# A streaming trunk step: places of the attention stage on Trainium2 laid out anew, and the samples' merges due later

## The chip, the core and the metric

The kernel runs on one core of a Trainium2 chip. The metric is device time in microseconds of one execution. A core has five engines that each work through their own queue in order: TensorE (PE, with its weight loads listed apart as PEld), VectorE (DVE), ScalarE (ACT), GpSimd (POOL) and SyncE (SP), which here issues nearly all DMA transfers.

## What is computed

One layer of a hybrid trunk for two groups of requests with shared weights: a prompt of 1024 tokens and 8 samples of 16 tokens each, 1152 tokens in all, model width 1024. The reference, cut:

```python
h = rms_norm(x, norm_g) * (1 + scale) + shift
q, k, v, z_att, z_ssd, xbc, dt_raw, gates = split(h @ w_in)
q, k = rms_norm(q per head), rms_norm(k per head)
o_att = attend(q, k, v)          # prompt: own chunk of 64 and the 8 before; samples: cache of 512 and own 16
att_branch = (o_att * silu(z_att)) @ w_att_proj
xs, bm, cm = split(silu(causal_dwconv(xbc)))
y = ssd_scan(xs, softplus(dt_raw), a, bm, cm) + d_skip * xs
ssd_branch = rms_norm(y * silu(z_ssd)) @ w_ssd_proj
out = x + gate * ((sigmoid(g_att) * att_branch + sigmoid(g_ssd) * ssd_branch) @ w_out)
```

There are 16 attention heads of 64, with a bias by relative position, and 32 SSD heads of 64 in 4 groups, state 128. Outputs are y, the new keys and values, the last convolution inputs and the SSD states.

## The kernel before, in words

**Dense work.** Each dense product is done as three fp16 matmuls (high part by high part, high by low, low by high; L412, L413 and L415, or L465 to L467 for q, k and v) into fp32 accumulation. A *job* is one set of weight columns: 128 output channels by 1152 tokens take 72 matmuls of 384 columns. Job weights come from DRAM into a *raw* place (`w_ahead`, L308: up to four loads ahead), and are split into a high half (ScalarE, L330) and a low half (VectorE, L331) in weight places; `level` (L322) also sums their squares. Before, there are four raw places (`L_RAW`) and six weight places (`L_W`), so three jobs' halves can stand at once. `w_next` splits the next job inside the present one; `w_done` frees the places.

**Stages.** After the start, there are eight *attention units* (two heads each), then the SSD stage (4 groups, 16 head pairs), then the projections and the output. A unit's dense generator makes q, k and v for nine token tiles (`dense_tok`), then the gate z of the unit after it. Beside it run three more generators. `prelude` normalizes and transposes q and k (L962 for the prompt, L978 for the samples). `prompt` does the attention of the prompt in the six `ROUNDS` of L1082, each with products of earlier tiles first and then scores of new ones. `sample` (L1145) does the samples in two halves of four.

**One prompt tile.** Scores (L1115, TensorE) go to PSUM, to the one `s` tile or to two of three `g` banks. VectorE adds the bias and takes the minimum of the negated scores (L1013). ScalarE takes the exponentials (L1010). VectorE normalizes and splits into two fp16 halves (L1045, L1046). A DMA transposes them (L1052). TensorE multiplies with the values (L1070), and VectorE merges with the gate (L1121). A tile's scores lie in *score places* `S`, in pairs with a second pair for the transposed halves: ten in the attention layout and four more in the far region, 14 in all.

**One half of the samples.** Four key loads (L1158) into the four places `K`; scores (L1168, L1171); minimum, exponential, L1177; a copy that separates the 16-bit halves of the words (ScalarE, L1189); a DMA transpose (L1190); a merge of the halves on VectorE (L1192); products (L1201) with values loaded into the same places `K` (L1185); a copy, a transpose (L1213) and the merge with the gate (L1219).

**Places.** All tiles lie in one arena with hand-written layouts that overlap in time: `L_ATT` for attention, `L_SSD` and `L_HEAD` for the SSD stage and its head, `L_TAIL` for the end. Behind them, from `E0` on, lies a far region: in attention it holds the four halves of V (`L_V`) and four score places, and otherwise up to six places of 1184 columns (`L_MORE`) that SSD and tail tiles take first. `alloc` takes, of the places of a kind that no live tile overlaps, the one longest free; without one, the generator waits.

**What sets the order.** `run` (L796) interleaves the generators at build time. It keeps a planner's clock, which every `yield` of a cost moves on. `until` and `pause` are due times on that clock: the transposed weights of a prompt tile are due `TURN` = 9000 ns after their scores are ready, and the samples' merge L1192 `TURN` after its DMA. When a generator finds no place, the planner's clock moves without dense work. The build then orders each engine's instructions once more; those under `late` or `keep` stay in program order. Due times order the program; they are not waits on the chip.

```python
nc.scalar.activation(planes(pt, 0, 5), words(p, 0, 5), AF.Copy)                                            # L1189
dma(p.ap.bitcast(U16).rearrange("p (i k) -> p i k", k=P), pt.ap.bitcast(U16), transpose=True)              # L1190
yield from pause(TURN)
nc.vector.tensor_copy(words(pt, 0, 5), planes(p, 0, 5))                                                    # L1192
```

```python
if (lay is L_SSD or lay is L_HEAD or lay is L_TAIL) and tag == "T" or lay is L_HEAD and tag == "Y":         # L233
    try:
        return Buf(arena, arena.alloc(L_MORE, "T", cols), cols)
```

## Time and profile before

| | us |
|---|---|
| three runs | 1839.16, 1843.87, 1847.39 (median 1843.87) |
| the profiled execution, its own time | 1841.84 |
| its span, first to last instruction | 1839.7 |
| TensorE busy | 1770.4 |
| VectorE busy | 1229.7 |
| ScalarE busy | 958.6 |
| GpSimd busy | 330.0 |

The profile is of one execution. Its page gives, for each engine, the busy time and its share of the span, and then the span in 40 equal slices of 46 us: a digit is the busy share in tenths, and PEclk is the clock that was granted to TensorE, in tenths of full speed. A row of the waits names the engine and line that waited, what ended the wait, the sum, the number of times and the longest. A row of the timeline gives start, duration, engine, line, operation and count, and in brackets the idle time just before it with what ended it. A row of the windows gives the stretch, its length, the busy time of PE, PEld, DVE, ACT and POOL with instruction counts, then the granted clock, the DMA share and GB/s. L12 is line 12 of the kernel before. Matmuls overlap, so the distance from one start to the next, not the duration of a row, is what one costs.

### The profile page before, as it was taken

To read this page: it belongs to the slowest core of one execution; us is meant where nothing else is said; L and a number is where in the kernel's file an instruction comes from. 1 tells how busy PE (TensorE), PEld (TensorE's weight loads), DVE (VectorE), ACT (ScalarE), POOL (GpSimd) and SP (SyncE) were. 2 spreads that over 40 slices of the span, in tenths; PEclk is the share of its full clock that TensorE was granted. 3 is DMA by queue.
4 is the path that set the end of the run, shared out by engine and by line. 5 is a ranking of instruction groups with operands and counts; after the bars stand their busy time and mean duration, and the time that the engine had idled before them with its cause. 6 is when DMAs were issued, how large, how long until landed. Compare 5 with 4: busy or idle time off the path is not lost. (4 is left out here: it accounts for less than half of the span.)

```text
span 1839.7 us, 35020 instructions
## 1 busy us (share of the span) xinstructions
PE 1770.4 (96%) x13821; PEld 1105.9 (60%) x13821; DVE 1229.7 (67%) x2327; ACT 958.6 (52%) x1903; POOL 330.0 (18%) x624
## 2 busy tenths in 40 slices
PE   7999999999999969999999999999999999999998
PEld 3655555555555546666666667666666656666664
DVE  6466766767677766777676868677764635887732
ACT  8765645555465547644655566356554613334520
POOL 0232322213123101211312222222222110000000
PEclk9999999999999979999999999999999999999999
DMA  9258778678678665443444445334466952331331
GB/s 382 76 132 215 169 193 202 151 208 195 150 221 189 164 159 150 139 138 112 113 141 120 133 132 176 129 114 112 145 177 208 345 172 99 110 98 50 98 122 54
DMA packets 266566, 284.88 MB, mean 155 GB/s; under 512 B 199628, under 2 KB 200664, under 8 KB 266392
## 3 DMA queue, kind: packets, MB, share of 16 engines
q1 hardware_dynamic: 257432, 253.90, 49.6%
q0 software_dynamic: 8960, 28.65, 4.2%
q8 instruction: 110, 1.80, 0.4%
q14 instruction: 64, 0.52, 0.1%
HBM read 192.70 MB, written 43.66 MB: 128 GB/s over the span
## 5 line engine op out<-in xcount | busy, mean ns | idle before, releaser
L412 PE MATMUL d<-arena 128*128 128x384 f16 x2172 | 709.5, 327 | 3.7 <-DVE arena L1423 3.5
L415 PE MATMUL d<-arena 128*128 128x384 f16 x2172 | 709.2, 327 | 0.0
L413 PE MATMUL d<-arena 128*128 128x384 f16 x2172 | 709.2, 327 | 0.0
L415 PEld LDWEIGHTS <-arena 128*128 128x128 f16 x2280 | 223.1, 98 | 147.7 <-issue 1.8
L412 PEld LDWEIGHTS <-arena 128*128 128x128 f16 x2280 | 223.4, 98 | 144.7 <-issue 6.3
L413 PEld LDWEIGHTS <-arena 128*128 128x128 f16 x2280 | 223.2, 98 | 142.4 <-issue 5.1
L322 ACT ACTIVATE arena<-arena 128x1024 bf16<-128x1024 f32 (+3 forms) x169 | 181.8, 1076 | 144.3 <-DMA arena<-in_wall_dram 122.1
L330 ACT ACTIVATE arena<-arena 128x1024 f16<-128x1024 f32 (+1 forms) x117 | 122.1, 1044 | 175.5 <-PE d L413 149.3
L465 PE MATMUL d<-arena 128*128 128x384 f16 (+1 forms) x568 | 186.6, 329 | 1.9 <-ACT arena L668 1.6
L466 PE MATMUL d<-arena 128*128 128x384 f16 (+1 forms) x568 | 186.4, 329 | 0.0
L467 PE MATMUL d<-arena 128*128 128x384 f16 (+1 forms) x568 | 186.3, 328 | 0.0
L331 DVE SCALAR_TENSOR_TENSOR arena<-arena 128x1024 f16<-128x1024 f32 (+1 forms) x117 | 148.9, 1273 | 53.2 <-ACT arena L330 53.0
L1010 ACT ACTIVATE arena<-arena 128x640 f32<-128x640 f32 (+3 forms) x144 | 100.9, 703 | 122.4 <-DVE arena L1013 122.3
L1452 ACT ACTIVATE arena<-arena 128x128 f32<-128x128 f32 x288 | 88.6, 387 | 50.9 <-DMA arena<-acs_d 50.8
L1264 DVE SCALAR_TENSOR_TENSOR arena<-arena 128x1176 f32<-128x1176 f32 x72 | 104.6, 1453 | 12.2 <-ACT arena L1261 11.6
L1046 DVE SCALAR_TENSOR_TENSOR arena<-arena 128x640 f16<-128x640 f32 (+4 forms) x128 | 87.4, 713 | 0.0
L465 PEld LDWEIGHTS <-arena 128*128 128x128 f16 x576 | 56.3, 98 | 51.6 <-issue 17.5
L938 POOL TENSOR_SCALAR arena<-arena 128x16 f32<-128x16 f32 (+1 forms) x24 | 7.5, 312 | 423.0 <-DVE arena L911 422.1
L467 PEld LDWEIGHTS <-arena 128*128 128x128 f16 x576 | 56.4, 98 | 37.4 <-issue 0.3
L466 PEld LDWEIGHTS <-arena 128*128 128x128 f16 x576 | 56.5, 98 | 35.6 <-issue 2.3
L1514 POOL TENSOR_TENSOR rarena<-rarena,arena 128x256 fp32r<-128x256 f32 x64 | 55.3, 878 | 73.8 <-PE g L1598 50.2
L1534 DVE SCALAR_TENSOR_TENSOR arena<-arena,g 128x64 f32<-128x64 f32 x224 | 46.4, 275 | 32.6 <-ACT arena L1530 30.6
(242 smaller groups left out, 2621.0 us busy)
## 6 DMA issues: line engine op xcount, KB each, us to landing
arena<-in_wall_dram SPq DMA_DIRECT2D x85, 512.0 KB
arena<-acs_d SPq DMA_DIRECT2D x32, 576.0 KB
arena<-in_kc_dram SPq DMA_DIRECT2D x64, 256.0 KB
arena<-in_vc_dram SPq DMA_DIRECT2D x64, 256.0 KB
arena<-in_wada_dram SPq DMA_DIRECT2D x24, 512.0 KB
arena<-in_xT_dram SPq DMA_DIRECT2D x16, 576.0 KB
arena<-eacs_d SPq DMA_DIRECT2D x32, 288.0 KB
gate_d<-arena POOLq DMA_DIRECT2D x48, 192.0 KB, 3.1
```

The costliest lines, as they stand in the source:

```text
L322: keep(nc.scalar.activation(junk[:, :n], x, AF.Square, scale=scale * n ** -0.5, accum_out=sums[:, c:c + 1]))
L330: keep(nc.scalar.activation(hi, x, AF.Copy, scale=scale))
L331: keep(nc.vector.scalar_tensor_tensor(lo, x, scale, hi, ALU.mult, ALU.subtract))
L412: nc.tensor.matmul(ps, hi.r[:, wc], kh.r[:, tok], start=k == 0, stop=False)
L413: nc.tensor.matmul(ps, hi.r[:, wc], kl.r[:, tok], start=False, stop=False)
L415: nc.tensor.matmul(ps, lo.r[:, wc], kh.r[:, tok], start=False, stop=k == nk - 1)
L465: nc.tensor.matmul(ps, kh.r[:, tok], wh, start=k == 0, stop=False)
L466: nc.tensor.matmul(ps, kh.r[:, tok], wl, start=False, stop=False)
L467: nc.tensor.matmul(ps, kl.r[:, tok], wh, start=False, stop=k == KT - 1)
L1010: nc.scalar.activation(p, p, AF.Exp, bias=sm_[:, 4 + e:5 + e], scale=-1.0, accum_out=sm_[:, 6 + e:7 + e])
L1264: nc.vector.scalar_tensor_tensor(yc, r.ap[:, j:j + n], w4[:, i, j:j + 1], yc, ALU.mult, ALU.add)
L1452: nc.scalar.activation(me[e].ap[:, cs], me[e].ap[:, cs], AF.Relu, scale=-1.0, bias=a4[:, c, hds[e]:hds[e] + 1])
```

## The change

From L226 on, line numbers are four higher in the changed kernel. The diff, with what only renumbers the layout left in:

```diff
@@ layouts (L199 to L225) @@
-    H0 = fixed[0] + 4 * 1024
+    NSLOT = 12
+    H0 = fixed[0] + 3 * 1024
-    V0 = W0 + 6 * 512
+    V0 = W0 + 4 * 512
-    E0 = Z0 + 2 * 1024 + 5 * NT + 12 * 640 + 4 * 512 + 2 * 256 + 2 * 128 + 3 * 84
+    E0 = Z0 + 2 * 1024 + 5 * NT + (NSLOT + 2) * 640 + 4 * 512 + 4 * 256 + 3 * 128 + 3 * 84
-    L_RAW = arena.set_layout(fixed[0], [("raw", 4, 1024)])
+    L_RAW = arena.set_layout(fixed[0], [("raw", 3, 1024)])
-    L_W = arena.set_layout(W0, [("w", 6, 512)])
+    L_W = arena.set_layout(W0, [("w", 4, 512)])
-    L_ATT = arena.set_layout(Z0, [("Q", 1, 16 * P), ("T", 5, NT), ("S", 10, 640), ("U", 2, 640), ("K", 4, 512), ("q", 1, 256), ("d", 1, 256),
-                                  ("k", 1, 128), ("p", 1, 128), ("n", 2, 36 + 3 * 16), ("t", 6, 14)])
+    L_ATT = arena.set_layout(Z0, [("Q", 1, 16 * P), ("T", 5, NT), ("S", NSLOT, 640), ("U", 2, 640), ("K", 4, 512), ("q", 2, 256), ("d", 2, 256),
+                                  ("k", 2, 128), ("p", 1, 128), ("n", 2, 36 + 3 * 16), ("t", 6, 14)])
-    L_MORE = arena.set_layout(E0, [("T", 6, 1184), ("H", 1, 1024)])
+    L_MORE = arena.set_layout(E0, [("T", 3, 1184), ("H", 1, 1024)])
+    n = (HCOLS - E0 - 3 * 1184 - 1024) // 1184
+    L_MORE["T"] = L_MORE["T"] + arena.set_layout(E0 + 3 * 1184 + 1024, [("T", n, 1184)])["T"]
     L_SSD["H"] = L_SSD["H"] + L_MORE["H"]
-    L_V = arena.set_layout(E0, [("v", 4, NP // 2)])
-    L_ATT["S"] = L_ATT["S"] + arena.set_layout(E0 + 4 * NP // 2, [("S", 4, 640)])["S"]
+    L_V = arena.set_layout(E0, [("v", 2, NP // 2), ("pad", 1, 160)])
+    L_V["v"] = L_V["v"] + arena.set_layout(E0 + 1184, [("v", 2, NP // 2)])["v"]
+    L_ATT["Q"] = L_ATT["Q"] + arena.set_layout(E0 + 1184 + NP, [("Q", 1, 2048)])["Q"]
@@ w_ahead (L308) @@
-        while not hold[0] and loaded[0] < len(parts) and len(wraw) < 4:
+        while not hold[0] and loaded[0] < len(parts) and len(wraw) < 3:
@@ sample (L1191) @@
-                yield from pause(TURN)
+                yield from pause(TURN + 4000)
```

In numbers, n comes out as 4. `Q`, where a unit's q and k of eight token tiles stand until they are transposed, gets a second place, in the far region behind V. Score places go from 14 (ten and four far ones) to twelve. The places `q`, `d` and `k` of `L_ATT` go from one to two. Raw places go from four to three, and loads ahead with them; weight places go from six to four, two jobs' halves. The far region's dense places go from six to seven; beside attention, those that neither V nor the score places nor the second Q overlap go from two to four. The planner's due time of the merge L1192 goes from 9000 to 13000 ns after its DMA. No instruction is added or removed on any engine; the planner and the ordering at build time place them anew.

## The prediction

> **What bounds the kernel now.** I read the page first: which engine fills the span, and in which slices it does not.

> ```profile
> PE 1770.4 (96%) x13821; PEld 1105.9 (60%) x13821; DVE 1229.7 (67%) x2327; ACT 958.6 (52%) x1903; POOL 330.0 (18%) x624
> PE   7999999999999969999999999999999999999998
> PEclk9999999999999979999999999999999999999999
> ```

> TensorE is busy for 96% of the span. Its work is the same after the change (the same matmuls stand in both programs as built, in another order), so the change can move only the idle 4% and the time at a lower clock. Both digits dip in one slice, the fifteenth. So next I read busy time by stretch: attention units 0 to 6, the end of the last unit, the SSD stage, the end.

> ```profile
> 60.00:620.00 560.00, 542.37 (x5046) 319.62 (x5043) 386.36 (x1023) 317.29 (x770) 147.70 (x298) 1.00 0.71 174
> 620.00:680.00 60.00, 41.95 (x416) 26.21 (x416) 43.60 (x100) 31.62 (x64) 5.09 (x12) 0.80 0.72 171
> 700.00:1450.00 750.00, 738.93 (x5521) 494.95 (x5520) 527.79 (x794) 416.95 (x788) 166.26 (x291) 1.00 0.48 146
> 1490.00:1830.00 340.00, 340.00 (x2102) 204.16 (x2099) 202.29 (x316) 109.63 (x145) 0.00 (x0) 1.00 0.29 95
> ```

> The first number after the length is TensorE's busy time. Idle: 17.6 us in units 0 to 6, 18.0 us in the 60 us at the end of attention, 11.1 us in the whole SSD stage, none after. Third, who ended these waits (TensorE's waits, for 100 to 620 and then for 620 to 680):

> ```profile
> PE s L1115 <- DVE arena L1013: 6.3, 6, 1.3
> PE g L1201 <- DVE arena L1192: 6.1, 6, 1.7
> PE s L1168 <- DMA arena<-in_kc_dram: 2.6, 4, 0.9
> ...
> PE g L1070 <- DMA arena<-arena: 0.8, 2, 0.5
> ```

> ```profile
> PE g L1070 <- DMA arena<-arena: 9.9, 4, 5.6
> PE g L1070 <- DVE arena L1013: 3.7, 1, 3.7
> PE s L1168 <- issue: 2.2, 1, 2.2
> PE g L1213 <- DVE arena L1121: 1.3, 1, 1.3
> ```

> In the units, scores (L1115) wait for VectorE to read the bank before, and the samples' products (L1201) for the merge L1192. At the end, the products L1070 wait for transposed weights. Fourth, the timeline: TensorE at that end, then VectorE in unit 1.

> ```profile
> 655.44 3.41 PE L1070 MATMUL g<-arena 128*64 128x128 f16 x60 [3.67 <-DVE arena L1013]
> 658.78 0.98 PE L1115 MATMUL s<-arena 64*128 64x320 f16 x6
> 659.56 1.01 PE L1115 MATMUL g<-arena 64*128 64x320 f16 x6
> 660.77 1.25 PE L1168 MATMUL s<-arena 128*32 128x512 f32 x4 [0.21 <-DVE arena L1013]
> 667.65 0.28 PE L1070 MATMUL g<-arena 128*64 128x128 f16 x1 [5.63 <-DMA arena<-arena]
> 673.24 0.31 PE L1070 MATMUL g<-arena 128*64 128x128 f16 x1 [2.44 <-DMA arena<-arena]
> 674.33 1.81 PE L1070 MATMUL g<-arena 128*64 128x128 f16 x29 [0.78 <-DMA arena<-arena]
> ```

> ```profile
> 202.50 0.89 DVE L1192 COPY arena<-arena 128x1280 uint16<-128x1280 uint16 x1 [4.75 <-DMA arena<-arena]
> 203.28 0.33 DVE L1013 CUSTOM_DVE_ANT_0 arena<-s,arena 128x128 f32<-128x128 f32 x1
> ```

> The last unit has run out of dense matmuls to put between scores and products: from the last scores (660.57) to the last weights (674.33) is 13.8 us of latency with nothing to cover it. In the units, L1192 stands at the head of VectorE's queue until its transpose lands; the L1013 that TensorE needs stands behind it.

> **The change, part by part.** For dense work I use 0.163 us a matmul:

> ```profile
> 647.68 0.33 PE L413 MATMUL d<-arena 128*128 128x384 f16 x1
> 649.30 0.33 PE L415 MATMUL d<-arena 128*128 128x384 f16 x1
> ```

> There are ten starts between them, 1.62 us. Distances come from TensorE's order as built, durations from this trace.

> *Places (L_MORE, L_V, second Q).* Beside attention, the head of the SSD stage could take only the two dense places of the far region that V and the four extra score places leave free; now it is four. In the order as built this shows in unit 7. Before, round 3's scores are followed by round 4's products without a dense matmul, and round 4's scores by round 5's products likewise. After, 52 dense matmuls stand ahead of the first half of round 4's products, 22 more ahead of the rest, and 83 (20 and 63) between round 4's scores and round 5's products: 83 x 0.163 = 13.5 us, with the samples' scores 15.9, against the 13.8 needed. In full units the same place has 84. So I take 15 of the 18.0 idle us as gone, 3 as left. Bounds: all gone; or half, if what is late next (the transposes, behind loads in SP's queue) grows by what the cover gains.

> With the idle time goes the lower clock:

> ```profile
> 620.00:630.00 10.00, 7.78 (x47) 4.02 (x47) 6.56 (x17) 7.29 (x16) 2.10 (x7) 0.85 0.50 132
> 650.00:660.00 10.00, 5.03 (x74) 4.16 (x73) 9.56 (x21) 4.51 (x7) 0.00 (x0) 0.72 0.98 234
> 660.00:670.00 10.00, 3.11 (x31) 1.33 (x27) 7.03 (x18) 2.90 (x7) 0.00 (x0) 0.67 0.78 185
> 670.00:680.00 10.00, 6.78 (x63) 4.36 (x60) 4.67 (x8) 4.91 (x13) 1.48 (x4) 0.59 0.82 189
> ```

> ```profile
> 676.36 0.53 PE L413 MATMUL d<-arena 128*128 128x384 f16 x1
> 676.68 0.53 PE L415 MATMUL d<-arena 128*128 128x384 f16 x1
> ```

> At 676 dense matmuls start 0.32 us apart, twice the 0.163. If clock is full or half, 0.85, 0.72, 0.67 and 0.59 are 3.0, 5.6, 6.6 and 8.2 us at half. TensorE worked through the first (3.0) and about two thirds (20.4 of 30) of its 14.9 us in the others: 13 us of work at half, so 6.5 us lost. I take 5 as regained, 1.5 as lost again in a gap that stays.

> [...]

> *Merges later (TURN + 4000).* The planner's due time of L1192 moves 4 us back, and with it all behind it in the samples' chain: 20 product steps (L1201), their copy and transpose, the release of four K places and of a U place, and so the four key loads of the next half on SP.

> ```profile
> DVE arena L1192 <- DMA arena<-arena: 54.3, 16, 5.0
> ```

> VectorE stood 54.3 us at 16 merges. As built, the first half's merge now stands behind at least the four L1013 that free the score bank in units 1 to 6 (before: ahead of all six), so the 6.3 us of L1115 waits should go. The second half's merge has moved past little more than one instruction and still stands ahead of L1121 and the next unit's L1013; its products have 15.3 to 21.2 us behind their scores, against 14.3 in units 0 to 5. Of those 6.1 us I take half, since the next scores now stand where these products stood. Cost of the moved key loads:

> ```profile
> 222.53 1.30 SPq L1158 DMA_DIRECT2D arena<-in_kc_dram  x3
> 228.25 0.62 PE L1168 MATMUL s<-arena 128*32 128x512 f32 x1 [0.59 <-DMA arena<-in_kc_dram]
> ```

> Last load to arrival is 4 to 5 us, and units 1 and 4 now leave about 6 us between the second half's products and the next samples' scores, where 15 stood. Bounds 0 and 4 us a unit; I take 1.

> *Twelve score places, pairs of q, d, k.* They let units run in another rhythm: dense work is spread unevenly. Scores of round 0 to products of round 2 have 8.3 and 9.5 us of TensorE work in units 1 and 4 (before 17.0), and round 1 to round 3 9.8 and 8.8 in units 3 and 6 (before 19.9). The trace shows no such short distance in a full unit. Bounds: nothing, as the products are spread over the arrivals (in unit 1 the 36 stand in four pieces between samples' scores); or the 13.8 us above less the distance: 5.5, 4.3, 4.0 and 5.0 in the four units, 19. I take 5, nearer to nothing, as query tiles 0 to 3 have one to four key blocks where tile 7, of the 13.8, has five.

> *Fewer weight and raw places.* A split then starts when the job before ends, one job later. Cover:

> ```profile
> 1148.63 1.06 ACT L330 ACTIVATE arena<-arena 128x1024 f16<-128x1024 f32 x1 [1.11 <-PE d L413]
> 1156.15 1.22 DVE L331 SCALAR_TENSOR_TENSOR arena<-arena 128x1024 f16<-128x1024 f32 x1
> ```

> Of the stage's 54 splits, paired row by row, this is the slowest from start to end, 8.7 us; a job lasts 72 x 0.163 = 11.7. Cost nothing. If the cover went, each late split would cost its lateness. Three raw places still load two jobs or more ahead.

> *SSD stage.* One place more, and as built the pairs stand evenly inside a group, most with 78 to 81 dense matmuls between them where 114 to 138 stood, and about 200 at group ends. VectorE has 527.8 us of work there in 750. I take 0; bounds -8 (most of the 11.1 us idle) and +10.

> Sum, against the profiled execution (1841.84, the span of 1839.7 and 2.1 around it; the runs' median is 1843.87): end of attention -15 - 5, waits at the merges -6.3 - 3, key loads +2, uneven units +5, SSD 0: -22. **1820 us.**

> **The rivals.**

> 1. *Uneven units wait.* The new short distances cost their upper bound, 19 instead of 5, and the key loads theirs, 8 instead of 2. For it: VectorE and SP work in order, and the DMA share is 0.71 there. Against: L1070 waited 0.8 us for transposes in all units 0 to 6, so 17.0 us of cover was ample. 1820 + 20 = 1840; at half the price, 1830.

> 2. *The end only moves.* Transposes queue behind loads (DMA share 0.98 at 650 to 660) and half the tail stays: 1820 + 10 = 1830. The change would then not do at the end what its places allow.

> 3. *Slower: weights late.* With two jobs' places, a split cannot hide behind two jobs. It decides when a split takes more than 11.7 us after the previous job. If VectorE's queue, fuller inside the closer pairs, adds 5 us to the 8.7 (four of its 1.3 us rows), a split is 2.0 us late; 20 of the 54 in the stage so, 40 us: 1860.

> ```profile
> L331 DVE SCALAR_TENSOR_TENSOR arena<-arena 128x1024 f16<-128x1024 f32 (+1 forms) x117 | 148.9, 1273 | 53.2 <-ACT arena L330 53.0
> L330 ACT ACTIVATE arena<-arena 128x1024 f16<-128x1024 f32 (+1 forms) x117 | 122.1, 1044 | 175.5 <-PE d L413 149.3 <-PE g L413 24.1 <-DMA arena<-in_wall_dram 1.5
> ```

> Against it: the two operations alone take 1.04 + 1.27 = 2.3 us, and ScalarE already waits 149.3 us for TensorE with the split, so it comes as soon as it may.

> **How the numbers follow.** Forecast 0.55; uneven units 0.20; the end only moves 0.12; weights late 0.13. Low end: both bounds at the good side, all of the tail (-24), all waits at merges (-12.4), nothing added: 1805, with a little of the SSD idle 1803. High end: rival 1 at its price and the SSD stage 2 us worse, 1842. That leaves out rival 3 and little else. A measurement of this kernel can tell about 0.5%, 9 us, from no change. Faster by more (below 1834.7): the forecast, half of rival 1, most of rival 2, 0.73. Within: 0.14. Slower: 0.13.

> **What would show it.** In the profile after, the fifteenth slice should be 9 for TensorE and clock, and 13 us between the last L1115 and the last L1070 of unit 7 should be full of d matmuls. L1115 should no longer wait for L1013 by 6 us; VectorE's 54.3 us at L1192 should be halved. Wrong if L1070 waits for the transposes by over 10 us in units 1, 3, 4, 6, or if d matmuls wait for L331 in the SSD stage.

## The result, and the profile after

The changed kernel takes **1855.69 us** (median of 20 runs, 1844.99 to 1864.97), the kernel before 1845.67 beside it (20 runs, 1839.16 to 1851.43): a ratio of 1.0053, 95% interval 1.0039 to 1.0067. It is 10 us slower; the forecast was 1820, and the range ended at 1842. The profiled execution of after took 1858.02 us with a span of 1856.2, against 1841.84 and 1839.7: these two differ by 16.5 us of span, since before's lies 4 us under its median and after's 2 us above.

TensorE's row and the two rows of slices of after:

```profile
PE 1774.5 (96%) x13821; PEld 1105.0 (60%) x13821; DVE 1225.4 (66%) x2327; ACT 957.6 (52%) x1903; POOL 362.6 (20%) x624
PE   7999998999989989999999999999999999999998
PEclk9999999999999999999999999999999999999999
```

TensorE is busy for 4.1 us more than before with the same matmuls, and idle for 12.4 us more. The dip of the fifteenth slice is shallower, 8 for 6, and the clock's digit there is 9 for 7; but the seventh and the twelfth slice have gone from 9 to 8. By stretch (units 0 to 6; the next 60 us; the SSD stage; the end):

```profile
60.00:620.00 560.00, 527.80 (x4880) 310.47 (x4879) 365.58 (x973) 304.19 (x742) 163.94 (x287) 0.98 0.71 170
620.00:680.00 60.00, 53.30 (x506) 31.37 (x505) 54.24 (x137) 33.03 (x72) 9.13 (x24) 0.97 0.66 159
700.00:1450.00 750.00, 729.27 (x5440) 487.08 (x5438) 520.50 (x788) 413.90 (x793) 174.14 (x290) 0.99 0.48 146
1500.00:1840.00 340.00, 340.00 (x2101) 204.25 (x2100) 206.06 (x320) 115.59 (x153) 0.00 (x0) 1.00 0.30 100
```

Idle in units 0 to 6: 32.2 us where 17.6 stood. At the end of attention 6.7 where 18.0 stood, at a clock of 0.97 where 0.80 stood. In the SSD stage 20.7 where 11.1 stood. So the end did get better, and more was lost on both sides of it. TensorE's waits in 100 to 620:

```profile
PE g L1074 <- DMA arena<-arena: 14.6, 11, 2.7
PE g L1205 <- DVE arena L1196: 5.9, 2, 3.8
PE g L1119 <- DVE arena L1223: 2.4, 2, 1.6
PE g L1074 <- DVE arena L1125: 2.2, 1, 2.2
```

Line numbers are four higher: L1074 is L1070, the products that wait for transposed weights: 0.8 us before, 14.6 now. The waits of L1119 (L1115 before) for L1017 (L1013), 6.3 us, are gone from the list. One such wait, in unit 2 (units are counted from 0, each from its first scores), on SP, then VectorE, then TensorE (`...` where rows are left out):

```profile
266.98 2.88 SPq L1194 DMA_TRANSPOSE arena<-arena  x1
272.92 0.33 SPq L1158 DMA_DIRECT2D arena<-in_bias_s_dram  x1
274.77 1.24 SPq L1056 DMA_TRANSPOSE arena<-arena  x1
276.12 0.52 SPq L316 DMA_DIRECT2D arena<-in_wall_dram  x1
276.73 1.24 SPq L1056 DMA_TRANSPOSE arena<-arena  x1
```

```profile
267.65 0.16 DVE L1042 RECIPROCAL arena<-arena 128x2 f32<-128x2 f32 x1
272.00 0.90 DVE L1196 COPY arena<-arena 128x1280 uint16<-128x1280 uint16 x1 [4.19 <-DMA arena<-arena]
272.79 0.15 DVE L1043 TENSOR_SCALAR arena<-arena 128x2 f32<-128x2 f32 x1
...
273.18 0.87 DVE L1049 TENSOR_SCALAR arena<-arena 128x512 f16<-128x512 f32 x2
273.97 0.74 DVE L1050 SCALAR_TENSOR_TENSOR arena<-arena 128x512 f16<-128x512 f32 x1
```

```profile
281.62 1.21 PE L1074 MATMUL g<-arena 128*64 128x128 f16 x23 [2.66 <-DMA arena<-arena]
...
284.77 0.53 PE L470 MATMUL d<-arena 128*128 128x384 f16 x1
285.09 0.44 PE L471 MATMUL d<-arena 128*128 128x384 f16 x1
```

The later merge (L1196, L1192 before) still stands on VectorE until its transpose lands, 4.19 us. Only what is behind it is another thing now: the normalization (L1042, L1043, L1049, L1050) of the tile whose weights TensorE needs next; its first instruction had run at 267.65, the next one runs at 272.79. The transposes leave at 274.77 and 276.73, and TensorE stands for 2.66 us. Behind the gap dense matmuls start 0.32 us apart, at half clock.

This wait and one of 2.33 us in unit 5 are the only two of the eleven with a merge that held VectorE for over 4 us in the 9 us before their transpose left. Both are at round 3's products, with 13.3 us of TensorE work behind round 1's scores where 18.0 stood before (worked out from the order, by the usual times of the next section). Of the 14.6 us, round 3 has 5.0, all in units 2 and 5, and round 4 has 8.2, in units 1, 3 and 4.

### The profile page after: what moved, and what is told of

It is laid out like the page before. It is cut to its first block, busy times and chain, and to the rows that moved or that the text cites. A ratio compares the mean times of both kernels' runs of the same rounds, so it can differ in the third digit from the quotient of the medians.

```text
span 1856.2 us, 35017 instructions
## 1 busy us (share of the span) xinstructions
PE 1774.5 (96%) x13821; PEld 1105.0 (60%) x13821; DVE 1225.4 (66%) x2327; ACT 957.6 (52%) x1903; POOL 362.6 (20%) x624
## 4 chain that ended last, share of the span: by engine, by line
PE 44%; DMA 7%; DVE 6%; ACT 5%; issue 2%; SPq 0%; POOL 0%; DVEq 0%; ACTq 0%; POOLq 0%
PE d L416 12%; PE d L417 12%; PE d L419 12%; DMA arena<-arena 3%; DMA arena<-acs_d 3%; ACT arena L1456 2%; DVE arena L1488 1%; DVE arena L1268 1%; PE g L416 1%; PE g L419 1%; PE g L417 1%; PE s L1557 1%; PE g L1529 1%; PE g L1577 1%; DVE arena L335 1%
## 5 line engine op out<-in xcount | busy, mean ns | idle before, releaser
L416 PEld LDWEIGHTS <-arena 128*128 128x128 f16 x2280 | 223.9, 98 | 152.5 <-issue 14.3
L417 PEld LDWEIGHTS <-arena 128*128 128x128 f16 x2280 | 223.7, 98 | 148.4 <-issue 11.6
L326 ACT ACTIVATE arena<-arena 128x1024 bf16<-128x1024 f32 (+3 forms) x169 | 181.8, 1076 | 195.2 <-DMA arena<-in_wall_dram 155.6
L334 ACT ACTIVATE arena<-arena 128x1024 f16<-128x1024 f32 (+1 forms) x117 | 121.9, 1044 | 153.2 <-PE d L417 124.6
L335 DVE SCALAR_TENSOR_TENSOR arena<-arena 128x1024 f16<-128x1024 f32 (+1 forms) x117 | 143.5, 1229 | 79.7 <-ACT arena L334 79.4
L1050 DVE SCALAR_TENSOR_TENSOR arena<-arena 128x640 f16<-128x640 f32 (+4 forms) x128 | 90.5, 735 | 0.0
L1017 DVE CUSTOM_DVE_ANT_0 arena<-s,arena 128x320 f32<-128x320 f32 (+4 forms) x128 | 58.8, 501 | 26.3 <-PE s L1175 15.5
L1074 PE MATMUL g<-arena 128*64 128x128 f16 x1440 | 52.2, 223 | 23.4 <-DMA arena<-arena 19.5
```

The lines of the kernel that those rows point to most:

```text
L326: keep(nc.scalar.activation(junk[:, :n], x, AF.Square, scale=scale * n ** -0.5, accum_out=sums[:, c:c + 1]))
L334: keep(nc.scalar.activation(hi, x, AF.Copy, scale=scale))
L335: keep(nc.vector.scalar_tensor_tensor(lo, x, scale, hi, ALU.mult, ALU.subtract))
L416: nc.tensor.matmul(ps, hi.r[:, wc], kh.r[:, tok], start=k == 0, stop=False)
L417: nc.tensor.matmul(ps, hi.r[:, wc], kl.r[:, tok], start=False, stop=False)
```

## The experiments

A measure for all of them. In each kernel I take the time at which TensorE reaches a landmark (the first scores of unit 0 and of unit 7, the first L1525 of the first and of the last SSD pair), less the usual start-to-start times of all matmuls ahead of it in the order as built (0.163 us for a dense one, and so on from the trace of before). What a stage adds to this difference is its *loss*: idle time, half clock, matmuls that don't overlap. It is worked out from one execution: a_n3 has TensorE's order of after up to 704 us, and the two differ by 8 us in the units. So the medians carry the verdicts. Kernels are named by their labels; "ratio" is to the kernel before, in the same set of runs; in these sets the median of the kernel before went from 1843.68 to 1846.55. The last three columns are losses in us.

| kernel | edit | median us | ratio (95%) | loss, units 0-6 | loss, end | loss, SSD |
|---|---|---|---|---|---|---|
| before | | 1845.67 | | 25.3 | 25.5 | 8.7 |
| after | the change | 1855.69 | 1.0053 (1.0039-1.0067) | 47.0 | 12.9 | 16.8 |
| b_far | before + far region | 1835.56 | 0.9949 (0.9930-0.9967) | 31.8 | 11.6 | 10.0 |
| b_turn | before + later merges | 1853.60 | 1.0044 (1.0027-1.0061) | 31.9 | 28.4 | 10.4 |
| b_w4 | before + fewer weight places | 1848.96 | 1.0020 (1.0009-1.0030) | 33.9 | 23.4 | 9.6 |
| a_qdk1 | after, single q, d, k | 1846.53 | 0.9998 (0.9983-1.0013) | 29.5 | 17.3 | 12.1 |
| a_n3 | after, six far places | 1848.70 | 1.0016 (1.0004-1.0027) | 38.8 | 12.0 | 9.1 |
| a_noturn | after, early merges | 1832.66 | 0.9935 (0.9923-0.9946) | 27.4 | 4.8 | 17.4 |
| a_qdk1_n3 | a_qdk1 and a_n3 together | 1841.22 | 0.9985 (0.9973-0.9997) | 31.6 | 17.5 | 9.4 |
| a_qdk1_noturn_n3 | the same, early merges | 1830.86 | 0.9927 (0.9914-0.9940) | 30.2 | 15.3 | 4.4 |
| a_noturn_n3 | early merges, six far places | 1841.64 | 0.9979 (0.9964-0.9995) | 27.2 | 16.1 | 11.5 |
| a_qdk1_noturn | single q, d, k, early merges | 1857.31 | 1.0067 (1.0051-1.0084) | 29.9 | 14.8 | 31.1 |
| a_noQ_noturn_n3 | a_noturn_n3, one Q | 1836.79 | 0.9947 (0.9931-0.9963) | 23.7 | 14.8 | 16.3 |
| a_noQ_qdk1_noturn_n3 | and single q, d, k | 1830.16 | 0.9910 (0.9893-0.9927) | 32.1 | 16.0 | 4.9 |
| a_turn06 | after, early merge in unit 7 | 1868.51 | 1.0107 (1.0092-1.0122) | 48.3 | 12.1 | 32.5 |
| a_turn7 | after, early merges in 0 to 6 | 1831.44 | 0.9917 (0.9898-0.9935) | 32.8 | 7.4 | 11.4 |
| a_qdk1_noturn_lev | a_qdk1_noturn, squares from the split half | 1839.20 | 0.9955 (0.9941-0.9969) | 32.3 | 9.8 | 16.3 |
| a_lev | after, the same | 1852.60 | 1.0039 (1.0026-1.0053) | 42.1 | 10.7 | 20.2 |
| a_noturn_lev | a_noturn, the same | 1834.23 | 0.9945 (0.9929-0.9961) | 23.2 | 15.0 | 17.0 |
| a_best_lev | a_noQ_qdk1_noturn_n3, the same | 1817.51 | 0.9866 (0.9842-0.9890) | 23.5 | 13.2 | 1.1 |

The row "before" is of one execution. b_far and b_turn have its order of TensorE in units 0 to 6 and lost 31.8 and 31.9 there: so before's 25.3 is a good execution of its kind, and about 32 is the fairer number to compare with.

**The parts alone.** b_far, the far region in another order:

```diff
-    L_MORE = arena.set_layout(E0, [("T", 6, 1184), ("H", 1, 1024)])
+    L_MORE = arena.set_layout(E0, [("T", 3, 1184), ("H", 1, 1024)])
+    L_MORE["T"] = L_MORE["T"] + arena.set_layout(E0 + 4 * NP // 2 + 4 * 640, [("T", 3, 1184)])["T"]
```

> The kernel before with the far region alone laid out in another order (three T places, H, three more T places behind V and the four score places), so that three instead of two dense places stay free beside attention; everything else as before. As built, units 0 to 6 keep TensorE's order of before and unit 7 gets dense matmuls ahead of rounds 4 and 5 (16.4 and 4.5 us of TensorE work between scores and products where 9.8 and 0.9 stood). Theory F (the free far places alone repair the end of attention, as step 1 of the prediction had it): idle at the end of attention falls from 18.0 to about 8 us, the clock there rises, SSD stage nearly unchanged (pairs 38 to 50 us apart as before): 12 us faster than before (6 to 18), about 1833. Rival E (the end only moves: a later start of the first SSD pairs gives back what attention gains): within 4 us of before.

Theory F holds: 1835.56, half a per cent faster than before. The stretch 620 to 700 in before and in b_far:

```profile
620.00:700.00 80.00, 61.95 (x575) 37.90 (x575) 50.76 (x109) 39.73 (x78) 7.39 (x16) 0.85 0.65 159
```

```profile
620.00:700.00 80.00, 69.59 (x668) 42.21 (x666) 56.16 (x122) 46.76 (x94) 8.76 (x19) 1.00 0.82 200
```

Idle 18.05 to 10.4 us, clock 0.85 to 1.00. A third dense place beside attention is enough for that.

b_turn, `pause(TURN)` to `pause(TURN + 4000)` in before:

> The kernel before with the later merges alone (TURN + 4000). TensorE's order in units 0 to 6 stays that of before; only VectorE's order moves. Theory M (the merge, still waiting 2 to 5 us for its transpose, now holds up other VectorE work, the normalization of the next tile ahead of its transposes): the 6.3 us of scores waiting at L1115 go, but products wait for transposes instead: from 2 us faster to 6 us slower than before. Rival U (the loss in the units comes from the uneven spread of dense work alone, and the later merge is a gain as step 2 of the prediction had it): 5 to 9 us faster than before, no new waits at L1070.

1853.60: slower by 8 us, at the bad end of theory M and beyond, but not by its mechanism. The first instruction that moves on any engine lies in unit 7: in full units the generator of the samples comes to the merge later than its due time anyway. So what the edit costs can only lie behind unit 6; by the losses, 4.6 us of it are seen there (end +2.9, SSD stage +1.7 against before's execution), and where the rest is stays open. In the stretch of the end TensorE's idle time (18.5 us) and its clock stay as they were:

```profile
620.00:700.00 80.00, 61.53 (x535) 35.04 (x534) 47.90 (x111) 36.03 (x73) 6.38 (x13) 0.85 0.65 157
```

b_w4, four weight and three raw places in before:

> The kernel before with four weight and three raw places, loads three ahead, all else at its place. As built, units 0 to 6 and the SSD stage behind its third pair keep their order. Step 4 of the prediction (cover 11.7 us against a slowest split of 8.7): within 3 us of before. Rival W (late weights): 8 us or more slower, with dense matmuls waiting for L331.

1848.96, 4 us slower than before (1.0020, 1.0009 to 1.0030): a little over step 4's 3 us. No dense matmul waits for L331. a_noQ_qdk1_noturn_n3 below has the same four and three places and is 5 us faster than b_far, so the price is not one of the places by themselves.

a_qdk1 (`("q", 1, 256), ("d", 1, 256)`, `("k", 1, 128)` in after) and a_n3 (`n = 3` in after):

> The changed kernel with one place each of q, d and k, as before, instead of two; twelve score places, second Q, far region, four weight places and later merges stay. As built, the units become even again (68.3 us of TensorE work each, 16 to 20 us between scores and products), the SSD stage keeps the order of the changed kernel. Theory U (uneven units, which come from the second places of q, d and k, cost 15 us of idle time and the half-clock periods behind the gaps): the units' idle time falls from 32.2 us (60 to 620) to about 17; time 15 to 20 us under the changed kernel, so 5 to 10 us faster than before. Theory M (the later merge itself blocks VectorE): the units stay near 28 us idle, time at most 5 us under the changed kernel, so 4 to 10 us slower than before.

> The changed kernel with three instead of four dense places behind H in the far region (six in the SSD stage, as before; three free beside attention). As built, units 0 to 7 keep the order of the changed kernel, and the SSD pairs stand about as before (38 to 50 us of TensorE work apart) instead of evenly 40 with long group ends. Theory S (the SSD stage's 8 us more come from the seventh dense place, by which the planner draws the pairs together): the loss within the SSD stage returns from 16.7 to about 9 us; time 8 us under the changed kernel, 0 to 3 us slower than before. Rival W (they come from four weight and three raw places, which this kernel keeps): as the changed kernel, 8 to 12 us slower than before.

1846.53 and 1848.70, 9 and 7 us under after. For a_qdk1 that lies between its two theories (15 to 20 us, or 5 at most). Its units are even again and their loss fell from 47.0 to 29.5, but the idle time in 60 to 620 hardly fell (560 less 529.7, 30.3 us, where theory U had 17): half clock (23.9 us of it in 60 to 620 in after, 13.7 here) and matmuls that overlap again (see the end) are a large part of the gain. a_n3's time is theory S's, and the loss of its SSD stage fell from 16.8 to 9.1.

**Undoing more than one.** a_noturn is after with `pause(TURN)`; the next two are a_n3 and a_qdk1 together, without and with the later merges.

> The changed kernel with the merges as early as before (TURN), all else changed. As built, the units get less uneven: 14.4 us or more of TensorE work between scores and products in units 0 to 6, where the changed kernel has 8.3 to 9.8 in four of them; but unit 7 now spreads its dense work badly (12.1 us ahead of round 2's products, 29.3 ahead of round 4's, 1.8 ahead of round 5's). Theory U (the short distances in units 1, 4, 3 and 6 are what costs in the units): units 0 to 7 lose some 30 us where the changed kernel loses 46.9, the end of attention some 6 us more than there: time 5 to 12 us under the changed kernel, 1844 to 1851. Rival P (the second places of q, d and k cost in any order, by more work in flight on VectorE): units as in the changed kernel, time as there or above, 1855 to 1862.

> The changed kernel with one place each of q, d and k, merges as early as before, and three dense places behind H; what stays of the change is the twelve score places, the second place of transposed queries, four weight and three raw places, and the far region's layout. Theory add (the three undone parts carry the whole loss, the rest is harmless): what is left is the gain at the end of attention, so as fast as the kernel before with the far region alone laid out anew: 1834 to 1840. Rival W (four weight places, or the second query place, or fewer score places in all, cost something too): 1843 or more.

> The same, but with the merges 4 us later as in the change. In the kernel before, the later merges alone cost 8 us, all of it behind unit 6, where they moved the order of the last unit, which had no dense work to cover it. Theory M7 (they cost only where the last unit is bare): here unit 7 has dense matmuls in front of every round, so 0 to 3 us above the kernel with the early merges. Rival M (they cost 8 us wherever they stand): 6 to 10 us above it, 1843 to 1848.

a_noturn: 1832.66, 23 us under after, far below what any theory gave, and faster than before. One line of the change costs more than the whole loss. a_qdk1_noturn_n3: 1830.86, faster than b_far and 3 us under theory add's range, so adding up seemed to hold. The later merges cost 10 us even there (1841.22), what rival M had said: M7 fell.

> The changed kernel with the merges as early as before and three dense places behind H; pairs of q, d and k, second query place, twelve score places and four weight places stay. If the seventh dense place costs the SSD stage by itself (theory S), taking it away is worth the same here as in the changed kernel, where it gave 7 us: 1832.7 less 7, so 1823 to 1828, the fastest so far. Rival: by the order as built, unit 7 has 5.8 us of TensorE work ahead of round 5's products and 12.1 ahead of round 2's, and the end of attention lost only 4.8 us without it, so what the SSD stage gains the end gives back: 1830 to 1836.

> The changed kernel with one place each of q, d and k and the merges as early as before; four dense places behind H stay. It is the fourth of a square: both (the changed kernel) 1855.7, later merges without pairs 1846.5, pairs without later merges 1832.7. If the two edits were independent, this one would be at 1846.5 - 23 = 1823.5. Theory U (only together do they make the units uneven; alone the later merges cost what they cost with three dense places, about 10 us): 1835 to 1840, so that the later merges cost 23 us with the pairs and about 8 to 10 without.

> As the first of these kernels, but without the second place of transposed queries. As built, the order from unit 7 on is the same; units 1 to 6 are even (68.3 us) instead of alternating between 60 and 72 us. If the second query place brings nothing by itself: within 3 us of the first. If it helps by letting a unit's queries be transposed earlier: 4 to 8 us slower than the first.

> What is left of the change here: twelve score places, four weight and three raw places, the far region with three dense places. TensorE's order in units 0 to 6 is that of the kernel before. Against the kernel before with the far region alone laid out anew (1835.6) it shows the price of fewer weight and score places: step 4 of the prediction says 0 to 2 us (1834 to 1838); the kernel before with four weight places was 4 us slower than before, which would give 1840.

Here adding up broke down. a_noturn_n3 is 9 us slower than a_noturn: the SSD stage gained 6, the end of attention lost 11, as the rival said and more. a_qdk1_noturn was expected at 1835 to 1840 and is slower than the change, 1857.31: it has the worst SSD stage so far (31.1). With a_qdk1_noturn_n3 it differs by one far place, and by 26 us, all of it in that stage. The second Q brought nothing (a_noQ_noturn_n3 is 5 us faster than the one with it, which neither expectation had). Fewer score and weight places cost nothing in a_noQ_qdk1_noturn_n3 (1830.16). So I took the stages one by one.

**The units.** `TURN + (4000 if u < 7 else 0)`, and `u > 6`:

> The changed kernel with the merges later in units 0 to 6 and as early as before in unit 7. As built, units 0 to 6 are those of the changed kernel, and the SSD stage has the order of the kernel with single places of q, d and k and early merges (1857.3), in which the stage lost 31 us. Theory U + order (the units' own order costs 12 to 17 us, the stage's own order costs what it cost there, and they add): 1869 to 1875, the slowest of all. Rival (the units' idle time comes from run to run, or is given back behind them): within 4 us of 1857.

> The changed kernel with the merges later in unit 7 alone. As built, units 0 to 6 are those of the kernel with early merges (14.4 us or more between scores and products, 1832.7); the SSD pairs stand as in the changed kernel. Theory U: the uneven units 1, 4, 3 and 6 cost 12 to 20 us, so without them 1836 to 1844. Rival M (the later merges cost behind unit 6, not in the units): 1850 to 1856, as the changed kernel.

1868.51 and 1831.44: theory U, on both sides (the second with a larger effect than expected). a_turn06 is a_qdk1_noturn with uneven units, 11 us slower; from 684 us on the two have the same order of TensorE, so this is the cleanest pair. a_turn7 is the change with less uneven units, 24 us faster; but its order differs from after's up to 894 us, and by the losses only 14 of the 24 lie in units 0 to 6, the rest at the end of attention and in the SSD stage. TensorE's waits in 100 to 620, a_turn06 and then a_turn7:

```profile
PE g L1074 <- DMA arena<-arena: 16.0, 12, 3.0
PE g L1205 <- DVE arena L1196: 5.4, 2, 3.2
```

```profile
PE g L1074 <- DVE arena L1125: 6.2, 4, 2.1
PE g L1119 <- DVE arena L1223: 5.8, 4, 1.9
PE g L1074 <- DMA arena<-arena: 4.9, 3, 4.0
```

Pairs of q, d, k and later merges are both needed for the uneven order. The four kernels with both in units 0 to 6 (after, a_n3, a_turn06, a_lev) lost 38.8 to 48.3 there, the sixteen others 23.2 to 33.9. At the products of rounds 3 and 4 of these units the four waited 11.2 to 15.4 us for transposes, the sixteen 0.8 at most. So these waits come with the uneven order and go with it. They do not follow the shortest distances (8.3 to 9.8 us of TensorE work from scores to products, at round 2 in units 1 and 4 and at round 3 in units 3 and 6): in after TensorE waited 0.4 us for transposes there, 2.2 us with two waits that the profile puts down to ScalarE.

Idle time alone does not carry the loss either. From the first scores of unit 0 to those of unit 7, worked out from the traces:

| kernel | TensorE idle, us | time at half clock | half of TensorE's busy time in it | busy at the samples' scores |
|---|---|---|---|---|
| before | 17.3 | 0 | 0 | 32.0 |
| after | 31.9 | 23.9 | 10.9 | 27.9 |
| a_turn7 | 29.4 | 17.1 | 7.9 | 20.5 |
| a_qdk1_noturn | 29.8 | 6.8 | 3.4 | 23.1 |
| a_turn06 | 31.0 | 27.3 | 13.3 | 27.9 |

The fourth column is an estimate of what half clock cost: in before and after dense matmuls start 0.32 us apart in it and 0.163 outside (medians). In the cleanest pair (the last two rows) idle time differs by 1.2 us, half clock by 9.9 and the samples' scores by 4.8 (see the end). The other units stand idle nearly as long, on other waits, but more of the uneven units' idle time falls together in one stretch of 3.41 us (see the end): they had 23.9 and 27.3 us at half clock, the others of the table 0 to 17.1.

**The SSD stage.** With seven far places a_qdk1_noturn lost 31.1 us. ScalarE, VectorE and TensorE in it:

```profile
1100.11 1.06 ACT L326 ACTIVATE arena<-arena 128x1024 bf16<-128x1024 f32 x1 [6.31 <-DMA arena<-in_wall_dram]
1101.07 0.19 ACT L326 ACTIVATION_READ_ACCUMULATOR arena<-arena 128x1 f32 x1
1101.17 0.26 ACT L1534 ACTIVATE arena<-g 128x128 f32<-128x128 f32 x1
```

```profile
1101.46 2.20 DVE L1538 SCALAR_TENSOR_TENSOR arena<-arena,g 128x64 f32<-128x64 f32 x11 [9.18 <-ACT arena L1534]
```

```profile
1102.84 1.41 PE L1577 MATMUL g<-arena 128*128 128x128 f32 x5 [3.52 <-DVE arena L1538]
```

ScalarE stands 6.31 us at the sum of squares of a weight that is still loading. A copy that needs no weight stands behind it, VectorE waits for the copy, TensorE for VectorE. The edit reads the rounded half instead, which exists only after the split:

```diff
-        level(b.ap[:, :w], SW, keep)
+        level(hi.r[:, c], 1.0, keep)
```

> The kernel with single places of q, d and k, early merges and seven dense places (1857.3, the SSD stage lost 31 us), with the sum of squares of each weight (L326) read from the rounded half that the split makes instead of from the loaded weight; the check that the sum serves stays, and so does everything else. In that kernel ScalarE stood 6.3 us at L326 for a weight load, and the state's copy L1534, which VectorE and then TensorE waited for, stood behind it. Theory L (in the SSD stage, ScalarE's wait for loads at L326, in front of L1534 and L1360, is what makes TensorE idle): the stage loses 15 us or less, time 1838 to 1846. Rival V (VectorE's own work is too much for pairs 40 us apart): 1853 to 1860.

> The changed kernel with the same edit (the sum of squares read from the rounded half). As built, the units keep their short distances. Theory L: the SSD stage's loss of 16.8 us falls to about 9, the units' stays: 1846 to 1851. Rival V: 1852 to 1859.

> The changed kernel with early merges (1832.7) and the sum of squares of each weight read from the rounded half. There units 0 to 7 lost 27 us, the end of attention 5, the SSD stage 17. Theory L: the stage falls to about 10, the rest stays, 1824 to 1829, the fastest so far. Rival: what the loads no longer hold up, other waits of the seven-place order do: 1830 to 1836.

> The kernel with twelve score places, four weight and three raw places, three far dense places beside attention and nothing else of the change (1830.2, the SSD stage lost 5 us), with the same edit. If ScalarE's wait for loads costs TensorE only in the order of seven places, this one is within 3 us of 1830. If it costs in any order: 1822 to 1826.

1839.20: 18 us, theory L by its time; the SSD stage lost 16.3, a little over the 15 expected. But a_lev gained 3 us, and not in the SSD stage; a_noturn_lev nothing (1834.23 after 1832.66); and a_best_lev, with six places, gained 13 (8 by the ratios, since the two ran in different sets), more than either expectation. In all four ScalarE no longer waits at L326 for weight loads. In the three with seven places the stage still lost 16.3 to 20.2 us, to other waits; a_noturn_lev, 690 to 1500:

```profile
PE d L416 <- ACT arena L1360: 6.7, 2, 4.6
PE d L416 <- DVE arena L1427: 5.1, 2, 4.4
PE g L1577 <- DVE arena L1582: 3.1, 1, 3.1
```

With six places it lost 1.1, where 4.9 stood; 8.6 us of a_best_lev's gain lie in the units instead (32.1 to 23.5), where executions of one order differ by as much, so what the edit brought there stays open. So the wait at L326 does cost in the SSD stage, and it explains most of one seven-place kernel. What seven places cost beyond it is not one wait: the pairs stand 40 us apart with long group ends, and TensorE waits there for whichever engine is late (ScalarE 6.7 us, VectorE 5.1 and 3.1 in the rows above). That the closeness of the pairs is the cause is argued from this, not shown; and a_noQ_noturn_n3 lost 16.3 us with six places.

**a_best_lev** beats both kernels: 1817.51 us, 0.9866 (0.9842 to 0.9890), with twelve score places, four weight and three raw places, six far places of which three are free beside attention, early merges, single Q, q, d and k, and the squares from the rounded half.

```profile
PE 1755.9 (97%) x13821; PEld 1102.8 (61%) x13821; DVE 1230.6 (68%) x2327; ACT 954.8 (53%) x1903; POOL 336.7 (19%) x624
```

## Why the prediction was wrong

The sum was -22 us; the two profiled executions differ by +16.5. By the losses: units +21.7 (the sum had -6.3 - 3 + 2 + 5 = -2.3), end -12.6 (-20), SSD stage +8.1 (0), start and rounding the rest. Against b_far and b_turn, which have before's order in the units, the units' loss is +15.

1. *End of attention* (-15 idle, -5 clock): mechanism right, size too large: -12.6 in after, -13.9 in b_far, where the medians give 10 us for this part alone. The idle time fell by 11.4 us in 620 to 700, not 15; one wait of 4.9 us for transposes stayed at round 4's products (the first row, of 620 to 700), and a new one of 2.7 us came at the head of the SSD stage (the second, of 700 to 740):

```profile
PE g L1074 <- DMA arena<-arena: 4.9, 1, 4.9
PE d L416 <- ACT arena L1245: 2.7, 1, 2.7
```

2. *Merges later* (-6.3, -3, +2): the step failed. The 6.3 us of scores waiting did go, but b_turn, where the later merges stand alone, keeps them (7.1 us), so it was not the later merges alone that took them away. VectorE's 54.3 us at the merge became 47.7, not half. And I costed the edit as moves within the units: alone it moves nothing there and costs 8 us all the same, which I had not priced. In other surroundings it cost 10 us (a_qdk1_n3), 23 (after against a_noturn) or, in unit 7 alone, nothing (a_turn7 against a_noturn), and a_qdk1 is 11 us faster with it than without.

3. *Uneven units* (+5, bounds 0 to 19): **this is the step that turned the sign.** That unevenly spread dense work would make L1070 wait for transposes came true: 14.6 us, 8.7 of them in units 1, 3 and 4 and none in 6, where the mark had asked for over 10. Where inside the units, and at what price, did not. At the places named, round 2 in units 1 and 4 and round 3 in units 3 and 6, TensorE waited 0.4 us for transposes (2.2 at most, see above), so the reason for a value near nothing, the few key blocks of the early tiles, fits there. The waits came at round 4 in units 1, 3 and 4 (12.9, 17.1 and 13.5 us of work behind the scores, where 17.2 stood) and at round 3 in units 2 and 5 (13.3 where 18.0 stood, behind a merge), which the step did not look at. That units 2 and 5 wait because of the merge is seen in the order of events; no run separates it from the shorter distance. Why unit 3 waits at round 4 is open.

The size: 11 us by the medians of the cleanest pair, 7 to 21 by the losses of the four uneven kernels, each against those with even units that differ from it in the pairs or in the later merges. That is near the top of the bounds, and over twice the value taken. The bound was latency less distance, once per unit; it left out what follows each gap. In before no half clock was granted in 60 to 620; in after 23.9 us were, in periods of 3.41 us or twice that, each behind a window of that length in which TensorE was busy for 0.16 to 0.46 of the time (see the end). Even units lost clock too, 0 to 20.5 us of it in the sixteen kernels against 17.1 to 27.3 in the four. The stretch behind the gap shown above:

```profile
280.00:290.00 10.00, 8.38 (x72) 4.84 (x74) 9.76 (x24) 2.86 (x8) 6.69 (x10) 0.83 0.70 131
```

The prediction had priced half clock at the end of attention, where it was to go, and not in the units, where the gaps were to come. I also put the uneven order down to the twelve score places and the pairs; it takes the pairs with the later merges, and twelve score places without pairs leave the units even.

4. *Fewer weight and raw places* (0): nearly right. 4 us in b_w4, nothing in a_noQ_qdk1_noturn_n3. Rival 3 (weights late) did not come in the form given: no dense matmul waited for a split. A late load did hurt, through ScalarE's queue (6.31 us at L326 in a_qdk1_noturn): something else stood behind it.

5. *SSD stage* (0, bounds -8 to +10): mis-sized, within its bounds: +8.1. I had read the closer pairs from the order as built and gave them no price. Taking the seventh place away gave back 3, 6, 8 and 27 us of that stage's loss in four pairs of kernels. Which wait it is that they cost stays open.

Rival 1 (uneven units wait, 1840) had the right stage and sign: its units come to -6.3 - 3 + 8 + 19 = +17.7. With the end and the SSD stage as measured it would have said 1840 + 7.4 + 8.1 = 1855.5, the median almost to the digit, and that is luck. It kept a gain at the merges that did not come, and its 8 us for the key loads did not come either: their waits went from 2.6 to 2.0 us.

## What to carry to other kernels

Where a planner sets the order, edits of places and due times don't add up: compare the order as built at every stage, and price each place where work that covered a latency has gone, not only the place that the edit was for. Price a gap with what follows it: in units 0 to 6 of after, 31.9 us of idle time went with 23.9 us at half clock, an estimated 10.9 us more. And look at what stands first in a queue with a wait of its own: L1043 stood behind a merge that waited 4.19 us, L1534 behind a weight load that was waited for 6.31 us, and neither needed anything from the transfer.

## What the runs showed of the hardware

```profile
135.13:138.55 3.42, 1.21 (x27) 0.85 (x25) 2.21 (x9) 0.59 (x1) 0.00 (x0) 1.00 0.32 58
138.55:141.96 3.41, 2.91 (x17) 1.44 (x17) 3.34 (x13) 3.41 (x12) 0.00 (x0) 0.50 0.24 87
933.85:937.27 3.42, 2.63 (x19) 1.39 (x15) 3.42 (x7) 0.00 (x0) 0.00 (x0) 1.00 0.96 274
937.27:940.68 3.41, 1.84 (x13) 1.45 (x14) 3.35 (x13) 2.26 (x6) 0.00 (x0) 1.00 0.89 242
940.68:944.09 3.41, 3.41 (x26) 2.45 (x24) 3.41 (x7) 3.41 (x13) 1.07 (x2) 1.00 0.24 84
363.83:367.24 3.41, 1.56 (x36) 1.25 (x37) 1.17 (x3) 0.00 (x0) 2.52 (x2) 1.00 1.06 195
367.24:370.65 3.41, 3.41 (x18) 1.46 (x13) 1.98 (x9) 1.74 (x4) 0.00 (x0) 0.50 1.08 274
```

**Busy time that is a wait.** The samples' scores are four matmuls on four strips of 32 columns. TensorE's busy time at them in 100 to 620, in before, after and a_best_lev:

```profile
L1168 PE MATMUL s<-arena 128*32 128x512 f32 x112 | 32.0, 605 | 2.6 <-DMA arena<-in_kc_dram 2.6
```

```profile
L1172 PE MATMUL s<-arena 128*32 128x512 f32 x112 | 27.9, 604 | 2.1 <-DMA arena<-in_kc_dram 2.0
```

```profile
L1171 PE MATMUL s<-arena 128*32 128x512 f32 x112 | 21.8, 605 | 0.0
```

The same 112 records of 0.605 us each overlap more where no key load is waited for: in 11 of the 28 groups of four in before, 6 in after and none in a_best_lev, every matmul starts over 0.2 us behind the one ahead, where others start 0.007 us apart. That is 10 us of busy time that the list of the matmuls' waits doesn't show; the list of the weight loads' waits has 12.1 us for the keys in before, but only 0.7 in after. All 12 kernels with 0.4 us or less of such waits of the matmuls have 21.8 to 23.7 us there (in 112 to 120 records), the others 27.9 to 32.0. That the late loads are the cause is read from this; no run moved them alone. In the prediction the key loads stood with +2 us; after gained 4 us there.
